# Where a convolution's running sum is kept: SBUF or a PSUM bank, in a decoder layer on one Trainium2 core

## The chip, the cores and the metric

One core of a Trainium2 chip runs the whole layer as one program. Five engines work side by side, each on its own queue in its own order: TensorE (PE) multiplies matrices and writes PSUM, VectorE (DVE) and ScalarE (ACT) do elementwise work and read and write both memories, GpSimd (POOL) does elementwise work in SBUF alone, and SyncE (SP) issues the transfers. PSUM has eight banks of 128 x 512 fp32. The metric is device time in microseconds (us) of one execution. The kernel before takes 3000.27 us (median of 3 runs, 2999.34 to 3004.11). A difference of under 0.2%, about 6 us, cannot be told from no change here.

## The reference

One decoder layer on 2048 tokens of width 1024. A normalised and modulated input is multiplied by one wide matrix, and the columns feed three mixers:

```python
h = rmsnorm(x, norm_mix_w[l]) * (1.0 + sc1) + sh1
proj = h @ w_in[l]
o_a = hgrn2_mixer(hq, hf, hi, hg, ...)     # gated linear recurrence, 4 heads of 128x128 state
o_b = dsa_mixer(sq, sk, sv, iq, ik, iw)    # index scores, top 256 keys, softmax attention
o_c = conv_module(cu, ...)                 # this change
mix = concat([o_a, o_b, o_c]) @ w_out[l];  x = x + g1 * mix
ff = square(relu(h2 @ mlp_w1[l])) @ mlp_w2[l];  x = x + g2 * ff
```

The convolution module is the part that is edited: `h = a * sigmoid(b)` on 256 channels, a causal depthwise convolution of 31 taps over the positions plus a bias, a LayerNorm over the channels, and a swish. So each output is a sum of 31 products of a shifted row with one weight per channel.

## The kernel before

The tokens go in four blocks of 512 (`NB`). For each block `in_block` runs 26 projection units: 23 of 24 matmuls 512 columns wide (L424) and 3 of 96 matmuls of 256 columns (L1290). Each operand is split into a high and a low part, so that a product is three matmuls. Nearly all units write one of two `mm` PSUM banks, which ACT and DVE take off. Then come the output projection of block 0 (L1314, `out_block`) and the MLP blocks, between which the other output projections lie. Call the matmuls of L424, L1290, L1314 and L1474 the wide ones: they are nearly all of PE's work.

Beside the projections run generators that are pumped a piece at a time by `step()`:

- `hgrn_gen`, the recurrence, one head of one block at a time, 16 in all, here numbered 0 to 15. A head is a chain: two score banks `pd` (L681, read at L685 and L687), six levels in each of which PE multiplies into a bank (L706, L714), DVE or ACT takes it into `at` (L708, L718) and DVE scales halves of q and k (L671, L672) that the next level reads; then a transpose of k (L728), the state update (L734, L739, L747), the outputs (L744, L746), a root mean square on ACT and POOL (L751, L252, L755), a transpose back (L759) and a last product on DVE (L761). All its banks have the tag `ax`.
- `conv_gen`, the convolution of one block, in two halves of 128 channels (`m`). Of the 31 taps, DVE adds 16 into `acc` (L585 starts it, L597 adds 15); the other 15 are multiplied by ACT, the first straight into `cside` (one buffer, L591) and 14 into `ctap` (one buffer, L594), which POOL adds to `cside` (L595). L602 adds the two sums. After both halves the LayerNorm takes an `ax` bank three times (L608, L620, L627).
- index scores, top-k and attention (L819 to L1024), and the modulation vectors (`ada_gen`, L196).

The PSUM banks in the first stage: two `mm`, two `at`, one `po`, and three rotating `ax` (`px["ax"]` is 3 there). In the MLP stage that pool is closed and its three banks are handed out again: one `ax` and two `ix`; the first user of each waits for the last reader of the bank's former tile.

The order of the instructions on each engine is not that of the source: a scheduler places them when the program is built, by the order of emission, by when buffers come free, and by its own estimate of durations. Each engine then runs its list strictly in order. So a change of a buffer moves instructions over the whole program.

Of the kernel before, what the change touches and what calls it, by code (L numbers as in the profile page):

```python
# [8 lines left out]
F32 = mybir.dt.float32  # L9
# [7 lines left out]
OP = mybir.AluOpType  # L17
# [3 lines left out]
P = 128  # L21
D = 1024
L = 2048
TB = 512
# [54 lines left out]
def trunk(ctx, tc, x, c, ada_w, ada_b, norm_mix_w, norm_mlp_w, w_in, hg_lb_logits,  # L79
# [3 lines left out]
    V, A, G, T = nc.vector, nc.scalar, nc.gpsimd, nc.tensor  # L83
# [14 lines left out]
    px = {"p": SP.enter_context(tc.tile_pool(name="psx", bufs=1, space=PSUM)), "ax": 3}  # L98
# [3 lines left out]
    def nm(s):  # L102
        uid[0] += 1
        return f"{s}_{uid[0]}"

    def dma(o, i):
        return nc.sync.dma_start(o, i)
# [5 lines left out]
        return pp.tile([P, 512], F32, tag="mm", bufs=2, name=nm("mm"))  # L113

    def ps_ax():
        return px["p"].tile([P, 512], F32, tag="ax", bufs=px["ax"], name=nm("ax"))

    def ps_ix():
        if px["ax"] == 3:
# [6 lines left out]
    def ps_xp(i):  # L126
        return {'0': ps_ax, '1': ps_mm, '2': ps_at, '3': ps_po}[XP[i]]()
# [3 lines left out]
    def ps_rot():  # L131
        turns[0] += 1
        return ps_mm() if turns[0] % 3 else ps_ax()
# [29 lines left out]
    crow = xp.tile([8, P], F32, tag="tf", bufs=2, name="crow")  # L163
    dma(crow, c[0].rearrange("(r p) -> r p", p=P))
    pt = ps_ax()
    T.transpose(pt[:, :8], crow, ident[:8, :8])
    cact = cst.tile([P, 8], F32, name="cact")
# [18 lines left out]
    def col(key, i=0, n=1):  # L186
        return cols[:, offs[key] + i:offs[key] + i + n]
# [62 lines left out]
    def rpow(dst, src, w, scale):  # L250
        G.tensor_scalar(dst, src, scale, EPS, op0=OP.mult, op1=OP.add)
        G.tensor_tensor(dst, dst, nhalf.to_broadcast([P, w]), OP.pow)  # L252
# [189 lines left out]
    hp = S1.enter_context(tc.tile_pool(name="hgrn", bufs=1))  # L442
# [9 lines left out]
    def st(tag, bufs, w=TB, dt=F32, shape=None):  # L452
        return hp.tile(shape or [P, w], dt, tag=tag, bufs=bufs, name=nm(tag))
# [126 lines left out]
    def conv_gen(b):  # L580
        accs = []
        for m in range(2):
            hc = conv[m]
            acc = hp.tile([P, TB], F32, tag=f"csg{m}", bufs=1, name=nm("cacc"))
            V.tensor_scalar(acc, hc[:, 0:TB], cvc[:, m, 0:1], col("cvb", m), op0=OP.mult, op1=OP.add)  # L585
            side = None
            for w in range(1, TAPS):
                if w % CT == 1:
                    if side is None:
                        side = hp.tile([P, TB], F32, tag="cside", bufs=1, name=nm("cside"))  # L590
                        A.mul(side, hc[:, w:w + TB], cvc[:, m, w:w + 1])  # L591
                    else:
                        tap = hp.tile([P, TB], F32, tag="ctap", bufs=CB, name=nm("ctap"))
                        A.mul(tap, hc[:, w:w + TB], cvc[:, m, w:w + 1])  # L594
                        G.tensor_tensor(side, side, tap, OP.add)  # L595
                else:
                    V.scalar_tensor_tensor(acc, hc[:, w:w + TB], cvc[:, m, w:w + 1], acc,  # L597
                                           op0=OP.mult, op1=OP.add)
                if w % 3 == 0:
                    yield 1300  # L600
            if side is not None:
                V.tensor_tensor(acc, acc, side, OP.add)  # L602
            accs.append(acc)
        yield 1200
        tot = st("cside", 1)
        G.tensor_tensor(tot, accs[0], accs[1], OP.add)
        pm = ps_xp(4)
        T.matmul(pm, o256.to_broadcast([P, P]), tot, start=True, stop=True)  # L608
        for m in range(2):
            V.tensor_tensor(accs[m], accs[m], pm, OP.subtract)  # L610
        sqs = []
        for m in range(2):
            sq = st("cu", 2)
            A.activation(sq, accs[m], AF.Square)
            sqs.append(sq)
        G.tensor_tensor(sqs[0], sqs[0], sqs[1], OP.add)
        yield 1500
        pv = ps_xp(5)
        for t in range(4):
            T.matmul(pv[:, t:t + 1], sqs[0][:, t * P:(t + 1) * P], ones[:, 0:1], start=True, stop=True)  # L620
        rc = hp.tile([P, 4], F32, tag="crs", bufs=1, name=nm("crs"))
        V.tensor_copy(rc, pv[:, :4])
        rpow(rc, rc, 4, 1.0 / 256.0)
        yield 1500
        rs = ps_xp(6)
        for t in range(4):
            T.matmul(rs[:, t * P:(t + 1) * P], rc[:, t:t + 1].to_broadcast([P, P]), ident, start=True, stop=True)  # L627
        for m in range(2):
            V.scalar_tensor_tensor(accs[m], accs[m], col("lnw", m), rs, op0=OP.mult, op1=OP.mult)
            sg = st("cu", 2)  # L630
            A.activation(sg, accs[m], AF.Sigmoid, bias=col("lnb", m))
            o = st("cu", 2)
            V.scalar_tensor_tensor(o, accs[m], col("lnb", m), sg, op0=OP.add, op1=OP.mult)
            dma(mx_d[b][6 + m], o)
        yield 3000
# [491 lines left out]
    def in_block(b, xts, nxt):  # L1127
        act = first_units(xts) if b == 0 else to_act(xts, a1, sh1, half if TM else None)
        for u, (pieces, ev, m) in enumerate(in_units):
# [38 lines left out]
            if ev is ev_ca and m == 1:  # L1168
                queues["conv"].append(conv_gen(b))
# [507 lines left out]
```

## Time and profile before

| | us |
|---|---|
| median of 3 runs | 3000.27 |
| the profiled execution | 3001.11 |
| its span, first to last instruction | 2999.4 |
| PE busy | 2810.5 (94%) |
| DVE busy | 1722.4 (57%) |
| ACT busy, POOL busy | 1297.8 (43%), 1265.8 (42%) |
| mean granted clock of PE | 0.972 |
| DVE in L597, 120 taps | 120.4 |
| POOL in L595, 112 taps | 164.3 |

PE is the busiest engine, so what counts is where PE stands idle or runs below its full clock. In a table by stretches of time, "us, busy (x)" gives for each engine the busy time and the count of instructions in the stretch, and "PEclk" the granted clock. A row of the waits says which PE instruction waited for which instruction of another engine: total, times, longest.

### The profile page before, as it was taken

Reading aid. Unit: us, or ns where it says so; the run is one execution under the profiler, and the core shown is the slowest. Engines: PE = TensorE matmul, PEld = TensorE weight load, DVE = VectorE, ACT = ScalarE, POOL = GpSimd, SP = SyncE. Lnnn points to the kernel's source line nnn. Section 1 sums busy time; section 2 is a strip of 40 time slices with the busy share of each in tenths; the row PEclk is TensorE's granted clock in tenths of the full one; section 3 lists DMA queues with packets and bytes.
Section 4 is the critical chain, followed back from the end, with each engine's and each line's share of the span. In section 5 each row is a group of like instructions: output and inputs, shape, how many; then the busy total and the mean of one; then the engine's idle time right before and its main releaser. Section 6 shows DMA issues by size and latency. Waiting matters only on the chain. (4 is left out here: it accounts for less than half of the span.)

```text
span 2999.4 us, 42837 instructions
## 1 busy us (share of the span) xinstructions
PE 2810.5 (94%) x14116; PEld 2325.2 (78%) x14116; DVE 1722.4 (57%) x3450; ACT 1297.8 (43%) x2706; POOL 1265.8 (42%) x1163
## 2 busy tenths in 40 slices
PE   6988989898899999999998999999999999999998
PEld 4877868786787877788776888877788888777777
DVE  7795487968446343747658646575944211244545
ACT  4445545435322324565546444443653333233333
POOL 7574143216313254566647422223532223334454
PEclk9999989999999998999998999999999999999999
DMA  8866656575644577899978966677786666676676
GB/s 280 273 203 210 214 185 203 188 238 181 210 167 152 180 253 230 255 296 285 294 234 271 313 218 202 218 219 227 248 290 208 220 223 213 213 269 229 225 235 210
DMA packets 428074, 688.61 MB, mean 230 GB/s; under 512 B 43383, under 2 KB 171452, under 8 KB 427836
## 3 DMA queue, kind: packets, MB, share of 16 engines
q1 hardware_dynamic: 427680, 685.67, 71.2%
q8 instruction: 112, 1.84, 0.3%
q14 instruction: 126, 1.03, 0.1%
q10 hardware_dynamic: 156, 0.07, 0.0%
HBM read 532.74 MB, written 152.84 MB: 229 GB/s over the span
## 5 line engine op out<-in xcount | busy, mean ns | idle before, releaser
L424 PE MATMUL mm<-ah,wk 128*128 128x512 f32 x1920 | 516.7, 402 | 15.6 <-DVE adrow L777 4.5
L424 PEld LDWEIGHTS mm<-ah,wk 128*128 128x128 f32 x1920 | 358.2, 191 | 90.0 <-DVE adrow L777 4.7
L318 POOL TENSOR_TENSOR wlo<-wraw,whi 128x512 fp32r<-128x512 f32 x210 | 290.2, 1402 | 168.5 <-ACT whi L317 104.7
L1008 POOL TENSOR_TENSOR pT<-L,pT 128x512 fp32r<-128x512 f32 (+3 forms) x160 | 198.0, 1239 | 295.7 <-ACT pT L1007 177.5
L826 DVE SCALAR_TENSOR_TENSOR s<-r,iw_s,s 128x512 f32<-128x512 f32 (+3 forms) x266 | 242.4, 911 | 112.9 <-ACT r L821 104.9
L424 PE MATMUL mm<-al,wk 128*128 128x512 f32 x960 | 266.3, 398 | 0.0
L978 DVE CUSTOM_DVE_ANT_0 L<-at,bias 128x512 f32<-128x512 f32 (+3 forms) x152 | 93.7, 619 | 219.6 <-PE at L976 180.7
L595 POOL TENSOR_TENSOR cside<-cside,ctap 128x512 f32<-128x512 f32 x112 | 164.3, 1467 | 109.9 <-ACT ctap L594 97.6
L424 PEld LDWEIGHTS mm<-al,wk 128*128 128x128 f32 x960 | 180.5, 192 | 36.5
L821 ACT ACTIVATE r<-ix 128x512 f32<-128x512 f32 (+3 forms) x256 | 133.0, 554 | 158.5 <-PE ix L819 117.8
L270 POOL TENSOR_TENSOR hl<-hr,hh 128x512 fp32r<-128x512 f32 x96 | 127.9, 1332 | 173.6 <-ACT hh L262 173.4
L1314 PE MATMUL mm<-wk,hh 128*128 128x512 f32 x640 | 198.6, 400 | 1.5 <-DMA wk<-wk_d 1.0
L424 PE MATMUL ax<-ah,wk 128*128 128x512 f32 x720 | 187.2, 393 | 1.4 <-ACT hc L1448 1.4
L317 ACT CAST whi<-wraw 128x512 fp32r<-128x512 f32 x210 | 121.3, 619 | 145.5 <-DMA wraw<-in_mlp_w_dram 46.6
L928 DVE TENSOR_SCALAR_CACHE_REDUCE cum<-s,ssm 128x384 bf16<-128x384 f32 (+13 forms) x112 | 165.4, 1477 | 10.4 <-POOL s L830 8.2
L424 PEld LDWEIGHTS ax<-ah,wk 128*128 128x128 f32 x720 | 134.1, 188 | 31.5 <-ACT hc L1448 1.9
L1006 ACT COPY L<-at 128x512 f32<-128x512 f32 (+3 forms) x160 | 83.0, 523 | 161.1 <-PE at L998 159.4
L1474 PE MATMUL mm<-wk,hc 128*128 128x512 f32 x588 | 147.7, 397 | 2.2 <-DVE acc L1482 2.1
L992 ACT ACTIVATE L<-L,nmx 128x512 f32<-128x512 f32 (+3 forms) x160 | 103.8, 651 | 104.8 <-DVE nmx L987 104.4
L1314 PEld LDWEIGHTS mm<-wk,hh 128*128 128x128 f32 x640 | 118.6, 189 | 28.2 <-DMA wk<-wk_d 1.8
L1474 PEld LDWEIGHTS mm<-wk,hc 128*128 128x128 f32 x588 | 109.6, 188 | 31.7 <-DVE acc L1482 5.7
L594 ACT ACTIVATE ctap<-hc,cvc 128x512 f32<-128x512 f32 x112 | 81.0, 723 | 107.4 <-POOL cside L595 106.9
(368 smaller groups left out, 6448.1 us busy)
## 6 DMA issues: line engine op xcount, KB each, us to landing
wk<-wk_d SPq DMA_DIRECT2D x776, 256.0 KB
wk<-wk_d SPq DMA_DIRECT2D x196, 512.0 KB
wk_d<-whi SPq DMA_DIRECT2D x210, 256.0 KB
wk_d<-wlo SPq DMA_DIRECT2D x210, 256.0 KB
wraw<-in_mlp_w_dram SPq DMA_DIRECT2D x68, 512.0 KB
kc<-sk_d SPq DMA_DIRECT2D x112, 256.0 KB
vc<-v_d SPq DMA_DIRECT2D x112, 256.0 KB
adw<-in_ada_w_dram SPq DMA_DIRECT2D x128, 128.0 KB
```

Source lines behind the costliest of these rows:

```text
L270: e.tensor_tensor(lo[:, i:j], src[:, i:j], hi[:, i:j].bitcast(F32), OP.subtract)
L317: A.copy(hi, src)
L318: G.tensor_tensor(lo, src, hi.bitcast(F32), OP.subtract)
L424: T.matmul(ps, ww[k], aa[k], start=(n == 0 and k0 == 0), stop=(n == len(order) - 1 and k1 == NK))
L595: G.tensor_tensor(side, side, tap, OP.add)
L821: A.activation(r[:, :w], ps[:, :w], AF.Relu, scale=32.0 ** -0.5)
L826: V.scalar_tensor_tensor(s[:, c0:c0 + w], r[:, :w], iw, s[:, c0:c0 + w], op0=OP.mult, op1=OP.add)
L928: V.tensor_scalar(dump, s, t, -AIM - i * STEP, op0=OP.is_ge, op1=OP.add, accum_out=d)
L992: A.activation(lt[:, :w], lt[:, :w], AF.Exp, bias=nmx, accum_out=sm[:, cb:cb + 1])
L1008: G.tensor_tensor(pT[:, :nt, 1], lv, pT[:, :nt, 0].bitcast(F32), OP.subtract)
L1314: T.matmul(ps, aa[f][:, tok * P:(tok + 1) * P], ww[i], start=(first and n == 0), stop=(last and n == 5))
L1474: T.matmul(bank[t], aa[:, k, t * P:(t + 1) * P], ww[k], start=(i in (0, 2, 4) and n == 0), stop=(n == 5), skip_group_check=True)
```

## The change

DVE's running sum of a half's taps is no longer an SBUF tile but a PSUM bank of a new tag `cx`, of which there is one. The sum of the two parts (L602) now reads that bank and writes an SBUF tile `total`, which the LayerNorm uses as it used `acc`. To make room, the recurrence and the LayerNorm rotate over two `ax` banks instead of three. The first tap and the 15 others of a half write the bank, the 15 also read it; the shifted rows `hc` stay in SBUF. The counts of instructions on DVE, PE, POOL and in the transfers are the same. In the MLP stage nothing of the source differs, but its three banks are now laid over two `ax` and one `cx`.

```diff
     def ps_ax():
-        return px["p"].tile([P, 512], F32, tag="ax", bufs=px["ax"], name=nm("ax"))
+        return px["p"].tile([P, 512], F32, tag="ax", bufs=min(px["ax"], 2), name=nm("ax"))
+
+    def ps_cx():
+        return px["p"].tile([P, 512], F32, tag="cx", bufs=1, name=nm("cx"))
...
         for m in range(2):
             hc = conv[m]
-            acc = hp.tile([P, TB], F32, tag=f"csg{m}", bufs=1, name=nm("cacc"))
+            acc = ps_cx()
             V.tensor_scalar(acc, hc[:, 0:TB], cvc[:, m, 0:1], col("cvb", m), op0=OP.mult, op1=OP.add)
...
-            if side is not None:
-                V.tensor_tensor(acc, acc, side, OP.add)
-            accs.append(acc)
+            total = hp.tile([P, TB], F32, tag=f"csg{m}", bufs=1, name=nm("cacc"))
+            V.tensor_tensor(total, acc, side, OP.add)
+            accs.append(total)
```

In the lists of the changed kernel the line numbers are 3 higher from L117 on (L597 is L600, L602 is L605, L728 is L731).

The first place is DVE's list at the convolution of the second block (tokens 512 to 1023). `cacc_4701` and `cacc_5240` are the running sums of the two halves, `hc` the shifted rows, `cvc` the weights. Before:

```order
L585 TENSOR_SCALAR cacc_5240<-hc_4690,cvc,cols 128x512
L597 SCALAR_TENSOR_TENSOR cacc_4701<-hc_4607,cvc,cacc_4701 128x512
L597 SCALAR_TENSOR_TENSOR cacc_5240<-hc_4690,cvc,cacc_5240 128x512
L597 SCALAR_TENSOR_TENSOR cacc_4701<-hc_4607,cvc,cacc_4701 128x512
L597 SCALAR_TENSOR_TENSOR cacc_5240<-hc_4690,cvc,cacc_5240 128x512
L597 SCALAR_TENSOR_TENSOR cacc_4701<-hc_4607,cvc,cacc_4701 128x512
L597 SCALAR_TENSOR_TENSOR cacc_5240<-hc_4690,cvc,cacc_5240 128x512
```

In the changed kernel `cx_4703` and `cx_5243` are the two sums, `cacc_5241` is `total`, `at`, `q`, `k` belong to the recurrence, and `slo` to a projection:

```order
L540 TENSOR_TENSOR slo_5051<-mm_5021,shi_5050 128x512
L605 TENSOR_TENSOR cacc_5241<-cx_4703,cside_4705 128x512
L711 COPY_PREDICATED at_4290<-lmask,ax_4509 128x64x4
L674 TENSOR_TENSOR q_3940<-q_3940,fb_4405 128x4x16x4
L675 TENSOR_TENSOR k_3815<-k_3815,fb_4405 128x64x4
L588 TENSOR_SCALAR cx_5243<-hc_4692,cvc,cols 128x512
```

Before, the taps of the two halves alternate. Now the second half's first tap (L588) stands behind the first half's total (L605), because there is one `cx` bank; it is so in all four blocks.

The second place is PE's list where the output projection of block 0 has ended and the MLP begins. `x_21..` are the normalised rows of block 0 that L278 transposes for the MLP; `ax` rows belong to head 15, the last of the recurrence. Before, the end of that head stands among these transposes:

```order
L728 MATMUL ax_11660<-ident,k_11084 128x128 x4
L278 MATMUL mm_11793<-ident,x_2171_11217 128x128
L278 MATMUL mm_11793<-ident,x_2172_11219 128x128
L278 MATMUL mm_11793<-ident,x_2173_11221 128x128
L278 MATMUL mm_11793<-ident,x_2174_11223 128x128
L278 MATMUL mm_11804<-ident,x_2171_11217 128x128
L278 MATMUL mm_11804<-ident,x_2172_11219 128x128
L278 MATMUL mm_11804<-ident,x_2173_11221 128x128
L278 MATMUL mm_11804<-ident,x_2174_11223 128x128
L734 MATMUL ax_11699<-v_10629,kt_11665 128x128 x4
L744 MATMUL ax_11708<-v_10629,at_11204 128x128
```

In the changed kernel it stands behind four units of the MLP (L427 is the wide matmul), and the unit behind it writes the MLP's own `ax` bank:

```order
L427 MATMUL mm_12091<-ah_11839,wlo_12031 128x512
L731 MATMUL ax_11668<-ident,k_11092 128x128 x4
L737 MATMUL ax_11707<-v_10636,kt_11673 128x128 x4
L747 MATMUL ax_11716<-v_10636,at_11212 128x128
L749 MATMUL ax_11716<-S_st_197,q_11170 128x128
...
L762 MATMUL ax_11738<-ident,hu_11727 128x128 x4
L427 MATMUL ax_11977<-ah_11762,whi_11912 128x512
```

So no wide matmul and no transpose of the input stands any more between L731 and L762 of head 15; the rows left out are six more of L747 and L749.

## The prediction

> **What bounds the kernel now.** I read the page's head, then the busy time by stretches, then PE's waits, then the groups of DVE and POOL, and last the timeline where the MLP begins.
>
> ```profile
> span 2999.4 us, 42837 instructions
> PE 2810.5 (94%) x14116; PEld 2325.2 (78%) x14116; DVE 1722.4 (57%) x3450; ACT 1297.8 (43%) x2706; POOL 1265.8 (42%) x1163
> ```
>
> PE bounds the whole: 189 us of the span are PE's idle time. The convolution runs in four short stretches, and the table of busy time, cut at their ends, shows another bound there. Columns: stretch, length, then busy us and count for PE, PEld, DVE, ACT, POOL, then the granted clock.
>
> ```profile
> 121.00:186.00 65.00, 53.85 (x240) 42.17 (x240) 65.00 (x100) 28.65 (x51) 44.24 (x33) 0.91 0.62 188
> 186.00:389.00 203.00, 185.52 (x1141) 161.53 (x1140) 118.96 (x324) 103.96 (x232) 78.70 (x88) 0.96 0.69 218
> 389.00:444.00 55.00, 42.06 (x197) 32.57 (x196) 54.16 (x91) 27.70 (x51) 29.97 (x26) 0.84 0.53 166
> 444.00:673.00 229.00, 208.91 (x1279) 181.78 (x1278) 169.12 (x465) 102.93 (x241) 61.16 (x73) 0.96 0.66 209
> 673.00:732.00 59.00, 48.09 (x243) 38.40 (x242) 54.76 (x91) 30.14 (x52) 37.38 (x25) 0.91 0.50 160
> 732.00:927.00 195.00, 181.55 (x1088) 157.57 (x1088) 81.67 (x186) 66.42 (x162) 48.40 (x48) 0.96 0.60 194
> 927.00:972.00 45.00, 38.95 (x188) 31.95 (x188) 44.72 (x60) 15.60 (x25) 20.52 (x16) 0.92 0.43 136
> 972.00:1117.00 145.00, 142.84 (x834) 123.40 (x833) 57.92 (x116) 47.31 (x113) 58.34 (x51) 0.98 0.63 205
> 1117.00:1146.00 29.00, 20.02 (x121) 16.17 (x119) 20.52 (x38) 10.68 (x19) 13.25 (x14) 0.71 0.45 158
> ```
>
> The convolution's stretches are rows 1, 3, 5 and 7: 224 us in which DVE is busy 218.6 (98%), PE 182.9, idle 41.1 (18%), at a clock of about 0.90. In the four stretches between (772 us) DVE is busy 427.7 (55%), PE 718.8, idle 53.2 (7%), at 0.96. So with the taps, DVE is what ends last, and PE pays: at the rate of the other stretches it would idle 15.4 us, so 25.6 are too many, and the lower clock (means weighted by PE's busy time) costs 182.9 x (1 - 0.896/0.964) = 12.9. Together **38.5 us is what a saturated DVE costs PE**. PE's waits over the first 1125 us name the path, the recurrence's chain through DVE. A tap stands in DVE's list between two links of this chain, and PE, in order too, holds its wide matmuls behind the next level. Columns: total, times, longest:
>
> ```profile
> PE ax L706 <- DVE k L672: 15.4, 9, 4.8
> PE ax L714 <- DVE k L672: 11.9, 8, 2.8
> PE ax L706 <- DVE q L671: 8.2, 3, 4.6
> PE ax L746 <- DVE sa L739: 6.5, 7, 3.0
> PE ax L728 <- DVE k L672: 4.8, 2, 4.6
> ```
>
> **The taps.** Their durations (minimum, median, maximum, ns), and the groups with their means:
>
> ```profile
> L597 DVE SCALAR_TENSOR_TENSOR cacc<-hc,cvc,cacc x120: 722/741/1875, 121.7 to 970.4; 128x512 f32<-128x512 f32 x120
> L629 DVE SCALAR_TENSOR_TENSOR cacc<-cacc,cols,ax x8: 732/740/749, 305.5 to 1103.4; 128x512 f32<-128x512 f32 x8
> L595 POOL TENSOR_TENSOR cside<-cside,ctap x112: 1262/1302/6887, 122.2 to 1002.1; 128x512 f32<-128x512 f32 x112
> L597 DVE SCALAR_TENSOR_TENSOR cacc<-hc,cvc,cacc 128x512 f32<-128x512 f32 x120 | 120.4, 1020 | 0.3
> L602 DVE TENSOR_TENSOR cacc<-cacc,cside 128x512 f32<-128x512 f32 x8 | 6.3, 783 | 0.0
> L610 DVE TENSOR_TENSOR cacc<-cacc,ax 128x512 f32<-128x512 f32 x8 | 5.1, 681 | 10.8 <-PE ax L608 10.8
> L585 DVE TENSOR_SCALAR cacc<-hc,cvc,cols 128x512 f32<-128x512 f32 x8 | 5.5, 682 | 0.0
> L287 DVE TENSOR_SCALAR ah<-mm,a,sh 128x512 fp32r<-128x512 f32 x48 | 38.2, 802 | 20.3 <-ACT tf L283 20.3
> ```
>
> A tap with both tensors in SBUF takes 741 ns at the median but 1020 on the mean; POOL's adds beside it are 1302 and (164.3 us over 112) 1467. L629 is the same operation with one tensor in PSUM, and never leaves 732 to 749. So a tap on the bank should take 0.741 us: 120 x (1.020 - 0.741) = 33.5 us, and L602, now like L610, 8 x (0.783 - 0.681) = 0.8: **34.3 us less DVE work**. POOL may gain up to 112 x 0.165 = 18.5 us, but the chain ACT to POOL of one half is long anyway, so I count nothing. The first tap moves between 0.68 and L287's 0.80: 1 us at most.
>
> [...]
>
> No row shows DVE writing PSUM, or reading and writing one bank. The bounds are 0.68 us (L610) and the slowest tap, 1.875; at 1.02 the gain is nil, at 1.875 DVE does 103 us more. I take 0.741, the row of the same operation.
>
> **Where the taps stand.** Before, both halves' 30 taps lie in the saturated stretch. With one bank the second half starts behind the first half's total, which waits for POOL's side sum; so about 60 x 0.741 = 44.5 us of DVE work leave these stretches for those behind them. What is a us of DVE worth to PE? Between 55% and 98% of DVE load lie 38.5 us of loss over 0.43 x 224 = 96 us of DVE time: 0.40. On that line moving work is neutral, and 34.3 saved is worth **13.7 us**. If the loss comes only close to saturation, moving counts too: the stretches fall to (218.6 - 120.4 + 44.5)/224 = 64%, and 38.5 x 34/43 = 30 us are the ceiling.
>
> **Two banks.** Inside a level the third bank is idle: a level's bank is read (L708) before the scaling that the next level needs. It bites at a head's change: L759's bank must be read by L761 before the next head's second `pd` bank is free, 0.75 us in the chain, 16 x 0.75 = 12 us if nothing covers it. In PE's built order the recurrence does fall back against the wide matmuls: head 3 starts behind 977 of them and not 897, head 8 behind 2056 (1920), head 12 behind 2952 (2812). PE does the same work in another order, so this is free while buffers last: `f` of a head needs the head three before it ended, and in that order the nearest case had 144 wide matmuls to spare and has 72, some 17 us at 8 in 1.9 us. I take nothing, and keep 0 to 12.
>
> **The start of the MLP.** What falls back must end here.
>
> ```profile
> 1117.26 0.63 PE L1314 MATMUL mm<-wlo,mh 128*128 128x512 f32 x2
> ...
> 1125.39 0.55 POOL L252 TENSOR_TENSOR rs<-rs,nhalf 128x1 f32<-128x1 f32 x1
> ...
> 1133.52 0.75 DVE L1375 TENSOR_SCALAR x<-x,rs 128x1024 f32<-128x1024 f32 x1
> ...
> 1138.82 1.11 PE L728 MATMUL ax<-ident,k 128*128 128x128 f32 x4
> ...
> 1141.31 1.06 PE L734 MATMUL ax<-v,kt 128*128 128x128 f32 x8
> ...
> 1145.55 0.39 PE L746 MATMUL ax<-sa,q 128*128 128x128 f32 x2
> ...
> 1145.97 0.50 PE L424 MATMUL mm<-ah,whi 128*128 128x512 f32 x1
> ...
> 1147.49 1.02 POOL L252 TENSOR_TENSOR hrs<-hrs,nhalf 128x4 f32<-128x4 f32 x1
> ...
> 1148.54 1.14 ACT L755 ACTIVATE hu<-ax,hrs 128x128 f32<-128x128 f32 x4
> ...
> 1153.78 0.75 DVE L761 SCALAR_TENSOR_TENSOR r<-ax,cols,gate 128x512 f32<-128x512 f32 x1 [6.94 <-PE ax L759]
> 1157.50 1.98 PE L424 MATMUL ax<-ah,whi 128*128 128x512 f32 x8
> ```
>
> From 1117.9 to 1146 PE has no wide matmul. The last row block's scale is ready at 1125.9, but DVE normalises it at 1133.5, behind levels of head 15. In the changed order the four L1375 stand ahead of that head: 7.6 us gained. But its end, L728 to L761, now has nothing of PE's beside it: 1138.8 to 1149.7 (L755), then about 0.6 for L759 (an estimate from L734's row) and 0.75 for L761, 12.2 us, of which about 5.3 are PE's own (L728 1.1, L734 1.1, eight pairs of 0.39); 6.9 lost. Net 0.
>
> **The sum.** 3001.11 is the profiled run, 1.7 over its span and 0.84 over the median. 3001.1 - 13.7 = 2987.4; less the 0.84, **2987 us**.
>
> **Rivals.**
> - *Saturation counts alone* (chance 0.13): 30 us gained, 2970. For it: DVE at 65.00 of 65. Against it: PE also waits for DVE in stretches where that is half idle.
> - *No change* (0.22): DVE gets lighter, but PE's list is in another order and waits as long at other places, or the bank write costs what the sharing cost: 3000, between 2995 and 3005. For it: the L706 and L714 waits also occur between the convolutions.
> - *Slower* (0.21): the recurrence, short of a bank, falls back so far that its end lies bare. Price: 16 x 0.75 = 12 us of bank waits and 6.9 at the MLP, less half of 13.7: 3012. It decides once L681 waits for L761 on PE, or the third MLP unit for L759. Against it: 72 wide matmuls of slack.
> [...]
>
> **Chances.** My forecast, 2980 to 2994, has 0.44. Taking all cases, the range is 2965 to 3011. A measurement here tells 0.2%, 6 us, from nothing; faster 0.55, same 0.21, slower 0.24.
>
> **What would show it.** L600 at a mean near 0.74 us with a narrow spread; POOL's L598 nearer 1.3; DVE well under 98% in the stretches with taps, and PE's idle time there under 18% and its clock over 0.9. Wrong if L600 is above 0.9, if PE's idle time up to the first MLP unit is as before, or if more than 10 us of idle PE stand around head 15's L731 to L762.

## The result, and the profile after

The changed kernel takes **2969.72 us** (median of four runs, 2959.47 to 2972.15) against 2999.81 for the kernel before: a ratio of 0.9888, 95% interval 0.9866 to 0.9911, faster by 30 us by the medians and 1.1% by the ratio. The forecast was 2987, in a range from 2965 to 3011. The profiled run of the changed kernel is the fastest of the four (2959.47, 10 us under their median), so differences between the two profiles come out near 42 us where the medians give 30.

In the rows of the changed kernel the tap is L600, the half's first tap L588, GpSimd's side add L598 and the sum of the parts L605. The head of its page:

```profile
span 2957.7 us, 42853 instructions
PE 2796.6 (95%) x14116; PEld 2310.3 (78%) x14116; DVE 1680.2 (57%) x3450; ACT 1297.0 (44%) x2704; POOL 1241.9 (42%) x1163
```

PE's idle time fell from 188.9 to 161.1 us, its busy time by 13.9. DVE is busy 42.2 us less, POOL 23.9 less. The group of GpSimd's adds (busy us, mean ns), and then every instruction on the bank (minimum, median, maximum, ns):

```profile
L598 POOL TENSOR_TENSOR cside<-cside,ctap 128x512 f32<-128x512 f32 x112 | 150.3, 1342 | 100.5 <-ACT ctap L597 88.3 <-ACT cside L594 9.9 <-DMA wk<-wk_d 1.1
```

```profile
L600 DVE SCALAR_TENSOR_TENSOR cx<-hc,cvc,cx x120: 730/748/757, 122.9 to 941.6; 128x512 f32<-128x512 f32 x120
L588 DVE TENSOR_SCALAR cx<-hc,cvc,cols x8: 793/802/814, 122.0 to 926.0; 128x512 f32<-128x512 f32 x8
L605 DVE TENSOR_TENSOR cacc<-cx,cside x8: 674/680/684, 174.0 to 958.6; 128x512 f32<-128x512 f32 x8
```

None of the 120 taps is longer than 757 ns; before, their mean was 1020 and the longest 1875. The adds beside them went from a mean of 1467 to 1342. The prediction's stretches with taps, from the first tap of a block to its last (columns as in the prediction: stretch, length, busy us of PE, PEld, DVE, ACT, POOL, granted clock), are now:

```profile
122.00:203.00 81.00, 73.68 (x381) 61.31 (x381) 73.15 (x174) 44.64 (x86) 58.44 (x50) 0.96 0.72 228
371.00:441.00 70.00, 61.88 (x311) 48.82 (x310) 63.30 (x115) 41.46 (x81) 40.55 (x39) 0.98 0.68 217
642.00:711.00 69.00, 59.55 (x286) 47.55 (x285) 63.66 (x122) 38.60 (x74) 37.96 (x35) 0.95 0.66 210
890.00:942.00 52.00, 51.81 (x259) 43.25 (x258) 41.16 (x69) 25.34 (x49) 28.89 (x24) 1.00 0.62 197
```

In these 272 us DVE is busy 241.3, still 89%, but PE idles only 25.1, 9% where it was 18%, at a clock of 0.95 to 1.00.

Where the time was won: cut both executions at the same wide matmuls (10284 in each; from the 96th to the 576th, the 1152nd to the 1344th, the 2016th to the 2112th, the 2880th to the 2976th). The four pieces hold most of the four convolutions, 107 of the 120 taps before. They give, before:

```profile
75.86:211.93 136.07, 120.22 (x611) 100.89 (x611) 110.01 (x209) 60.37 (x117) 84.20 (x65) 0.94 0.78 244
383.63:466.63 83.00, 68.22 (x334) 54.91 (x333) 74.86 (x130) 42.51 (x84) 45.38 (x40) 0.90 0.61 191
677.75:723.08 45.33, 34.73 (x181) 27.60 (x180) 41.58 (x68) 21.80 (x40) 28.94 (x19) 0.89 0.48 154
938.88:973.14 34.26, 28.21 (x137) 22.60 (x135) 34.04 (x48) 11.92 (x21) 13.95 (x10) 0.90 0.38 120
```

and after:

```profile
75.49:194.46 118.97, 112.79 (x603) 95.13 (x603) 88.11 (x206) 62.03 (x119) 77.58 (x65) 0.99 0.89 276
364.66:435.01 70.35, 62.23 (x315) 49.59 (x313) 59.85 (x109) 38.57 (x78) 38.19 (x39) 0.98 0.70 220
649.18:684.60 35.42, 31.70 (x146) 24.85 (x144) 32.52 (x68) 22.44 (x47) 18.45 (x17) 0.95 0.58 186
900.80:928.07 27.27, 27.08 (x137) 22.75 (x136) 17.74 (x34) 14.94 (x32) 14.45 (x13) 1.00 0.57 177
```

Together 298.7 us became 252.0: 46.7 won in these pieces, and 5 given back elsewhere. Of the 46.7, 29.1 are PE's idle time (length less PE's busy time: 47.3 before, 18.2 after), and 17.6 its busy time, whose granted clock went from 0.89 to 0.94 up to 0.95 to 1.00. Part of this is work that moved: after the change the pieces hold 74 taps, since the second halves come later, and 62 fewer of PE's small matmuls. Still, the stretches with taps idle less although they are longer, so the gain lies where the prediction put it; it is over twice the forecast size (30 us by the medians against 13.7).

PE's waits over the first 1125 us, as the prediction showed them of before (waiting line, released by; total, times, longest). After:

```profile
PE mm L427 <- ACT k L647: 11.5, 3, 5.6
...
PE ax L709 <- DVE k L675: 8.4, 10, 2.2
...
PE ax L749 <- DVE sa L742: 3.5, 5, 1.5
...
PE ax L684 <- DVE r L764: 3.0, 7, 1.5
...
PE ax L709 <- DVE q L674: 2.2, 2, 1.1
...
PE ax L731 <- DVE k L675: 1.9, 3, 0.8
PE ax L717 <- DVE k L675: 1.5, 3, 0.7
```

The five rows on the recurrence's chain that the prediction quoted were 46.8 us; the same five are 17.5 here. The bank wait that the two banks bring (L684 for L764) is 3.0. These five rows are a sign and not a measure of the time: in the runs below they are 34.6 in a kernel that is 44 us faster than the one before (no adds), and 35.5 in one that is 19 us slower (two banks alone).

One place shows what a tap was. The timeline of before, DVE and POOL side by side (start, duration):

```profile
135.09 1.32 POOL L595 TENSOR_TENSOR cside<-cside,ctap 128x512 f32<-128x512 f32 x1 [0.84 <-ACT ctap L594]
135.36 1.59 DVE L597 SCALAR_TENSOR_TENSOR cacc<-hc,cvc,cacc 128x512 f32<-128x512 f32 x1
136.37 3.12 POOL L318 TENSOR_TENSOR wlo<-wraw,whi 128x512 fp32r<-128x512 f32 x2
...
137.21 1.15 DVE L671 TENSOR_TENSOR q<-q,fb 128x256 f32<-128x256 f32 x1
138.29 1.48 DVE L672 TENSOR_TENSOR k<-k,fb 128x256 f32<-128x256 f32 x1
```

The tap begins 0.27 us behind the add and ends 0.54 behind the add's end, 0.85 us later than 0.74 would have taken it: it stood for most of the add. The next POOL operation (L318) meets the recurrence's own two products, L671 and L672, here 1.15 and 1.48 us; L672 is L675 in the changed kernel, and takes 0.41 in the next rows. Over all taps of before, the 38 beside which GpSimd has no instruction take 728 to 753 ns; the 68 that have one of its adds beside them take 1182 on the mean, up to 1875, and make 30 of the 33.6 us that the taps stand over 741. Why the two stretch each other, no row shows. The same kind of place after:

```profile
131.77 1.30 POOL L598 TENSOR_TENSOR cside<-cside,ctap 128x512 f32<-128x512 f32 x1
131.85 0.74 DVE L600 SCALAR_TENSOR_TENSOR cx<-hc,cvc,cx 128x512 f32<-128x512 f32 x1
...
132.83 0.51 DVE L674 TENSOR_TENSOR q<-q,fb 128x256 f32<-128x256 f32 x1
133.27 0.41 DVE L675 TENSOR_TENSOR k<-k,fb 128x256 f32<-128x256 f32 x1
```

The tap runs inside the add, neither is lengthened, and when the recurrence's products come the add is nearly over. The 71 taps of the changed kernel that have an add alone beside them take 730 to 757 ns.

### The profile page after: what moved, and what is told of

Read it like the earlier page. It is cut to its first block, busy times and chain, and to the rows that moved or that the text cites. A ratio compares the mean times of both kernels' runs of the same rounds, so it can differ in the third digit from the quotient of the medians.

```text
span 2957.7 us, 42853 instructions
## 1 busy us (share of the span) xinstructions
PE 2796.6 (95%) x14116; PEld 2310.3 (78%) x14116; DVE 1680.2 (57%) x3450; ACT 1297.0 (44%) x2704; POOL 1241.9 (42%) x1163
## 4 chain that ended last, share of the span: by engine, by line
PE 38%; DMA 5%; DVE 4%; POOL 2%; issue 1%; ACT 1%; SPq 0%; POOLq 0%; DVEq 0%; ACTq 0%
PE mm L1317 10%; PE mm L427 8%; PE ax L427 6%; PE ax L1317 5%; PE mm L1477 4%; PE po L1013 1%; PE at L979 1%; PE at L1001 1%; DMA wk<-wk_d 1%; PE at L1317 1%; PE ix L822 1%; DMA tr<-in_mlp_w_dram 1%; DMA xo<-x_d 1%; DMA wraw<-in_mlp_w_dram 1%; DMA out_dram<-xo 1%
## 5 line engine op out<-in xcount | busy, mean ns | idle before, releaser
L427 PE MATMUL mm<-ah,wk 128*128 128x512 f32 x1920 | 517.3, 401 | 15.1 <-ACT k L647 5.9
L427 PEld LDWEIGHTS mm<-ah,wk 128*128 128x128 f32 x1920 | 358.3, 191 | 90.0 <-ACT k L647 6.9
L427 PE MATMUL mm<-al,wk 128*128 128x512 f32 x960 | 262.1, 395 | 0.0
L427 PEld LDWEIGHTS mm<-al,wk 128*128 128x128 f32 x960 | 178.9, 190 | 36.0
L598 POOL TENSOR_TENSOR cside<-cside,ctap 128x512 f32<-128x512 f32 x112 | 150.3, 1342 | 100.5 <-ACT ctap L597 88.3
L427 PE MATMUL ax<-ah,wk 128*128 128x512 f32 x720 | 187.0, 393 | 1.5 <-ACT hc L1451 1.5
L427 PEld LDWEIGHTS ax<-ah,wk 128*128 128x128 f32 x720 | 134.0, 188 | 31.2 <-ACT hc L1451 1.9
L1317 PE MATMUL ax<-wk,hh 128*128 128x512 f32 x384 | 123.4, 400 | 0.9 <-DMA wk<-wk_d 0.5
```

The costliest lines, as they stand in the source:

```text
L427: T.matmul(ps, ww[k], aa[k], start=(n == 0 and k0 == 0), stop=(n == len(order) - 1 and k1 == NK))
L1317: T.matmul(ps, aa[f][:, tok * P:(tok + 1) * P], ww[i], start=(first and n == 0), stop=(last and n == 5))
```

## The experiments

Four explanations were set against one another. **Work**: PE is held up by the amount of VectorE's work in these stretches, so any us less is worth something between 0.4 (the prediction's line) and 1. **Order**: the second half's taps moved behind the first's total, and PE's list changed. **Chain**: GpSimd's shorter adds release ScalarE, which has one tap buffer and waits in order. **Collisions**: VectorE and GpSimd stretch each other, and the stretching costs, on whichever instruction it falls. Ratios are against the kernel before, run on the same chip.

**The banks alone (order).**

```
 before, ps_ax:
-        ... tag="ax", bufs=px["ax"]
+        ... tag="ax", bufs=min(px["ax"], 2)
```

> The kernel before with two rotating banks for the recurrence and nothing else; the convolution's sum stays in SBUF. If the taps' change gave the 30 us, two banks alone give nothing: 2995 to 3015, and the end of head 15, bare as in the changed kernel, costs up to 11 us there. The rival, that the changed order of PE's work (which two banks also bring) gave the gain, expects 2970 to 2985.

3018.7 us, ratio 1.0063 (1.0046 to 1.0079): 19 us slower, 4 more than the top of what was expected. Two banks, and the order that PE's list takes with them, give nothing; alone they cost.

**The order of the halves, without the bank.**

```
 after, conv_gen:
-            acc = ps_cx()
+            acc = hp.tile([P, TB], F32, tag="csg1", bufs=1, name=nm("cacc"))
...
-            total = hp.tile([P, TB], F32, tag=f"csg{m}", bufs=1, name=nm("cacc"))
+            total = acc if m else hp.tile([P, TB], F32, tag="csg0", bufs=1, name=nm("cacc"))
```

> The changed kernel with its running sum in one SBUF tile for both halves, in place of the bank: the second half still begins behind the first one's total, two banks stay, but the taps again have two inputs in SBUF. If the moved half is what counts, the time is near the changed kernel's: 2970 to 2980. If the shorter taps count (L600 at 748 against 1020), it is near the kernel before or above: 2995 to 3010, with the taps' mean back at 0.95 to 1.05 us, or somewhat lower where fewer of POOL's adds stand beside them.

3002.55 us, ratio 0.9999 (0.9986 to 1.0013). Moving the half is worth the 19 us that the two banks cost, and no more; the rest of the way to the changed kernel, 33 us (0.0111 of 3000), is the bank's. The taps were longer than before:

```profile
L600 DVE SCALAR_TENSOR_TENSOR cacc<-hc,cvc,cacc 128x512 f32<-128x512 f32 x120 | 129.8, 1082 | 1.4
```

**Less work, with the contention left as it is.** Four of the 15 taps that VectorE adds in each half are left out, once in the kernel before and once in the kernel with one SBUF sum:

```
+                    if w not in (4, 12, 20, 28):
                         V.scalar_tensor_tensor(acc, hc[:, w:w + TB], cvc[:, m, w:w + 1], acc, ...)
```

> The kernel before with 4 of the 15 VectorE taps of each half left out (32 instructions of a mean 1.02 us in all, 32.6 us; this part of the convolution is missing), and no other change. If a us of VectorE in these stretches is worth a us to PE, 2968 to 2972; by the 0.40 of the prediction, 2987; if it is hidden, 3000.

> One SBUF tile for both halves' sum and two banks (2995 to 3007), with 4 of 15 VectorE taps of each half left out (this part of the convolution is missing): 32 instructions of 1.08 us, 34.6 us less VectorE work, the contention stays. If the order of the halves decides what a us of VectorE is worth, 2970 to 2978 (0.8 a us, as from this kernel to the changed one). If the long taps are the cost, leaving some out gives as little as in the order before: 2994 to 3000.

2996.82 us, ratio 0.9981 (0.9970 to 0.9992), in the one; 3006.32, ratio 1.0017 (1.0001 to 1.0034), in the other. Over a quarter of these taps is gone, and 6 us are won or 5 lost. The groups, first from the kernel before, then from the one with one sum:

```profile
L598 DVE SCALAR_TENSOR_TENSOR cacc<-hc,cvc,cacc 128x512 f32<-128x512 f32 x88 | 87.5, 1009 | 0.2
```

```profile
L601 DVE SCALAR_TENSOR_TENSOR cacc<-hc,cvc,cacc 128x512 f32<-128x512 f32 x88 | 103.6, 1177 | 1.2
```

In the second the mean of the remaining taps rose from 1082 to 1177. DVE's whole busy time fell by 23.3 us in the one (1722.4 to 1699.1) and by 24.7 in the other (1730.3 to 1705.6), about 0.75 for each tap left out and not the 1.02 and 1.08 that they had taken: the standing stayed, on other instructions. The work explanation does not fit here, and neither does the prediction's way of counting; a us of VectorE that is saved by doing less is worth a quarter of a us in the one kernel and nothing in the other.

**More and less work on the bank.** The same four taps done twice, or left out, in the changed kernel:

```
-                    V.scalar_tensor_tensor(acc, hc[:, w:w + TB], ...)
+                    for _ in range(2 if w in (4, 12, 20, 28) else 1):
+                        V.scalar_tensor_tensor(acc, hc[:, w:w + TB], ...)
```

> The changed kernel with 4 VectorE taps of each half done twice (32 more instructions of 0.748 us, 23.9 us; these taps count double in the output). If a us of VectorE is worth a us to PE there, 2992 to 2996; by 0.40, 2979; if the moved half has left VectorE room, 2970.

> The changed kernel with 4 of the 15 VectorE taps of each half left out (32 instructions of 0.748 us, 23.9 us of VectorE work; this part of the convolution is missing). With SBUF sums, leaving the same taps out gave -6 us in the order before, and +4 us beside the one SBUF sum. If VectorE's work as such still holds PE up now that the taps meet nothing (by the 14 us that 23.9 us more cost), 2956. If only the stretching by collisions counts, nothing again: 2966 to 2972.

Twice: 2984.11 us, ratio 0.9946 (0.9929 to 0.9962), 17 us more than the changed kernel's 0.9888 for 24 us of taps. That is more a us than the prediction's 0.40, and the work explanation would have it so; but the standing rose as well, by 18 us in the table further down, and no run separates the two. Left out: ratio 0.9916 (0.9900 to 0.9932), five runs from 2973 to 2989; that is 8 us **more** as well, though the two intervals just overlap. Neither explanation had expected a loss. The profile shows where the saved 23.9 us went:

```profile
PE 2817.4 (94%) x14116; PEld 2329.9 (78%) x14116; DVE 1687.7 (56%) x3418; ACT 1302.0 (44%) x2708; POOL 1234.0 (41%) x1163
```

```profile
L676 DVE TENSOR_TENSOR k<-k,fb 128x256 f32<-128x256 f32 x96 | 62.7, 653 | 0.0
```

With 32 instructions fewer, DVE is busy 7.5 us *longer* (1687.7 against 1680.2). The taps left are as short as in the changed kernel (749 ns); others got longer, among them the recurrence's k product, whose mean went from 592 ns in the changed kernel,

```profile
L675 DVE TENSOR_TENSOR k<-k,fb 128x256 f32<-128x256 f32 x96 | 56.8, 592 | 0.0
```

to 653, and PE's waits for that chain came back:

```profile
PE ax L710 <- DVE k L676: 11.9, 9, 3.4
...
PE ax L718 <- DVE k L676: 9.0, 7, 3.3
PE ax L685 <- DVE r L765: 8.8, 4, 5.3
```

One reading is that a tap on the bank keeps GpSimd's adds away from the recurrence. The records do not show it: of the 224 products L674 and L675, 35 have an add beside them in the changed kernel and 32 of their counterparts here, the adds got shorter (1323 ns against 1342), and of the 11 us that the products gained 8 lie beside GpSimd's other work. This profile is of an execution of 2989.49 us and the changed kernel's of one of 2959.47, 30 us apart where the ratios give 8, so a part of what differs lies between executions. Why less work cost time here is open.

**Half on the bank.** The first half's sum in `cx`, the second's in SBUF, so that the halves alternate as before:

```
 after, conv_gen:
-            acc = ps_cx()
+            acc = hp.tile([P, TB], F32, tag="csg1", ...) if m else ps_cx()
...
-            total = hp.tile([P, TB], F32, tag=f"csg{m}", ...)
+            total = acc if m else hp.tile([P, TB], F32, tag="csg0", ...)
```

> The changed kernel with only the first half's running sum in the bank; the second half's is one SBUF tile, so that the halves no longer share a buffer and stand side by side as before, and only half of the taps (60) have two inputs in SBUF. So far: one SBUF tile for both halves and two banks gave 2995 to 3007 (as before), the bank 2970, both halves side by side with two banks 3019. If the shorter taps are what counts, half of them give half the way from 3019 to 2970: 2990 to 3000. If one half behind the other is needed as well, it stays at 3010 to 3020.

2988.1 us, ratio 0.9968 (0.9945 to 0.9991): 28 us better than two banks alone, about half of the way to the changed kernel. Both kinds of tap stand in one execution, between the same neighbours. Where one of GpSimd's adds alone is beside them, 33 on the bank take 745 ns on the mean and 28 in SBUF 978:

```profile
L600 DVE SCALAR_TENSOR_TENSOR cx<-hc,cvc,cx x60: 729/744/797, 121.1 to 927.5; 128x512 f32<-128x512 f32 x60
L600 DVE SCALAR_TENSOR_TENSOR cacc<-hc,cvc,cacc x60: 717/743/1780, 133.4 to 935.2; 128x512 f32<-128x512 f32 x60
```

**Three banks with the sum in one of them.**

```
 after, ps_ax:                          conv_gen:
-        ... bufs=min(px["ax"], 2)     -            acc = ps_cx()
+        ... bufs=px["ax"]             +            acc = ps_ax()
```

> The changed kernel with three rotating banks as before, and the running sum in one of them (no bank of its own): the recurrence has two while a sum lies there and three at other times, and the end of head 15 need not lie bare. If two banks cost the recurrence what they cost alone (19 us), much of it comes back: 2945 to 2960. If they cost nothing beside the sum in PSUM, 2965 to 2975. If the rotation makes a level wait for a whole sum, slower than 2980.

2966.59 us, ratio 0.9896 (0.9864 to 0.9928): not to be told from the changed kernel. A third bank, which the recurrence has whenever no sum lies in it, is worth nothing that shows.

**GpSimd's adds taken away.** From the kernel before, once without the adds, and once with two fills of the tap's buffer in their place:

```
 e8:                                                e11:
-  G.tensor_tensor(side, side, tap, OP.add)        -  G.tensor_tensor(side, side, tap, OP.add)
                                                   +  G.memset(tap, 0.0)
                                                   +  G.memset(tap, 0.0)
```

> The kernel before without GpSimd's 112 adds of the side taps (these taps are missing from the output), nothing else moved: VectorE's taps keep two SBUF inputs, but what they met beside them is gone. If GpSimd's adds are what lengthens them, the taps' mean falls from 1.02 to 0.74 to 0.80 us, 26 to 34 us less VectorE work. Time: by the 0.17 us per us that leaving taps out showed, 2994 to 2996; if a long tap itself (up to 1.9 us) is what PE waits for, 2965 to 2975.

> The kernel before with each of GpSimd's 112 side adds replaced by two fills of the tap's buffer with zeros (the side taps are missing from the output): the chain from ScalarE to GpSimd and back over the one buffer stays, at a similar length, but GpSimd reads nothing there. Leaving out the adds gave 2954. If the collisions are the cost, the taps fall to 0.75 to 0.85 us and the time to 2950 to 2965. If the chain over GpSimd is the cost, 2990 to 3000.

2954.12 us, ratio 0.9853 (0.9818 to 0.9888), without; 2955.15, ratio 0.9836 (0.9815 to 0.9857), with the fills. VectorE does all its taps from SBUF in both, in the order before and with three banks. The fills keep the loop from ScalarE to GpSimd and back, though shorter (118.6 us of POOL, where the adds were 164.3); ScalarE waits 76.0 us for them, and it costs nothing that shows:

```profile
L594 ACT ACTIVATE ctap<-hc,cvc 128x512 f32<-128x512 f32 x112 | 81.0, 723 | 76.5 <-POOL ctap L596 76.0
...
L595 POOL MEMSET ctap<- 128x512 f32 x112 | 59.6, 532 | 89.2 <-ACT ctap L594 89.0
L596 POOL MEMSET ctap<- 128x512 f32 x112 | 59.0, 527 | 5.1
```

A fill, which writes SBUF and reads nothing, stretched no tap here: the 76 taps that have only fills beside them take 722 to 758 ns. Two taps, the first beside a fill and the second beside L318:

```profile
130.25 0.73 DVE L598 SCALAR_TENSOR_TENSOR cacc<-hc,cvc,cacc 128x512 f32<-128x512 f32 x1
130.35 0.52 POOL L595 MEMSET ctap<- 128x512 f32 x1
...
133.34 3.45 POOL L318 TENSOR_TENSOR wlo<-wraw,whi 128x512 fp32r<-128x512 f32 x2
...
135.58 1.76 DVE L598 SCALAR_TENSOR_TENSOR cacc<-hc,cvc,cacc 128x512 f32<-128x512 f32 x1
```

The taps' means are 834 ns without the adds and 801 with the fills, not 741, since GpSimd's other work still meets them, as L318 does in the last two rows (the tap takes 1.76 us). GpSimd also has less to do in both, 162 and 57 us of its busy time, and what that alone is worth no run separates.

**ScalarE released from the adds (chain).** The side taps take the two `cu` buffers in place of the one `ctap`:

```
 before, conv_gen:
-  tap = hp.tile([P, TB], F32, tag="ctap", bufs=CB, name=nm("ctap"))
+  tap = st("cu", 2)
```

> The kernel before with two buffers in place of one for ScalarE's side taps, so that ScalarE, which works in order, can write the next tap while GpSimd still adds the last; the sum stays in SBUF. L594 waited 106.9 us for GpSimd's adds. If these waits, and what they hold up behind them on ScalarE, are what the long adds cost, then half of the gain at least: below 2985. If the cost is that VectorE and GpSimd stretch each other, the adds and the taps stay as long as before (taps 1.0 us, adds 1.4 to 1.5) and the time stays at 2995 to 3005.

3015.86 us, ratio 1.0040 (1.0024 to 1.0055): slower. ScalarE's wait fell from 106.9 to 66.9 us, and the taps' mean rose from 1020 to 1113 ns:

```profile
L594 ACT ACTIVATE cu<-hc,cvc 128x512 f32<-128x512 f32 x112 | 79.9, 723 | 67.0 <-POOL cside L595 66.9
...
L597 DVE SCALAR_TENSOR_TENSOR cacc<-hc,cvc,cacc 128x512 f32<-128x512 f32 x120 | 132.0, 1113 | 0.2
```

Forty us less waiting on ScalarE won nothing, and with the fills 76.0 us of it cost nothing that shows: the chain does not explain the gain.

**An attempt at a better kernel.** In the changed kernel the end of head 15 (L731 to L762) stands on PE behind four products of the MLP with nothing beside it. Here the first four take `mm` banks only, and the end stands among their matmuls:

```
 after, ps_rot:                        and behind px["ax"] = AXB:
+        if px.get("hold", 0):         +    px["hold"] = 4
+            px["hold"] -= 1
+            return ps_mm()
```

> The changed kernel with one more edit: the first four products of the MLP take their banks from mm alone, so that PE's list has the end of head 15 (L734 to L765 here) among their matmuls and not bare behind them. From the 3600th to the 3648th wide matmul the changed kernel had lost 9.3 us against the kernel before. If that was the bare end, 2960 to 2964; if the wait only moves behind, 2970.

2974.94 us, ratio 0.9913 (0.9894 to 0.9932): no gain, if anything a loss. By the 3648th wide matmul its profile is 2.5 us ahead of the changed kernel's, by the 3800th 8.6 behind: what the start gained was lost right behind it, and why is open. No version that does the whole layer's work was clearly faster than the changed kernel.

**All runs on one scale.** For each DVE instruction up to the MLP's first product, take what it lasted beyond the bound of the shortest tenth of its kind (same source line, operation and shape, over all the kernels here), and add up. This *stretch* is an estimate, worked out from the records of the profiled runs. Beside it, how many us of taps were added or left out (32 by 0.73 or 0.75), and the time by the ratio:

```
kernel                        stretch  plain work   time against before
before                          164        0              0
two banks alone                 161        0            +19
two tap buffers                 165        0            +12
one SBUF sum                    164        0              0
fewer taps, before              162      -23             -6
fewer taps, one SBUF sum        161      -23             +5
half on the bank                137        0            -10
more taps, after                134      +24            -16
fewer taps, after               145      -24            -25
sum in one of three banks       138        0            -31
changed, MLP starts on mm       124        0            -26
changed                         116        0            -34
no adds                          86        0            -44
fills for adds                   78        0            -49
```

A line through zero has a slope of 0.61 us of time per us of stretch, with a scatter of 9 us about it; the plain work beside it has no effect that these runs could tell. The two kernels with the least stretch, taken alone, give 44 us for 78 (no adds) and 49 for 86 (fills), that is 0.56 and 0.57 a us; by these the changed kernel's 48 us less are worth 27 to 28. That the stretch goes with the time over all these kernels is a correlation; that most of it comes of GpSimd's adds, and that time is won when they are gone, is what the runs without them show.

## Why the prediction was right, and where it was mis-sized

**The taps: right.** L600's mean is 748 ns, forecast 741; the narrow spread was forecast too. L605 took 680, L588 802, both as the rows of before had it. A tap that reads and writes the bank takes 7 ns more than one in SBUF (748 against 741, both medians; the 38 in SBUF beside which GpSimd has nothing take 740 on the mean). L600 above 0.9 us, by which the prediction would have been wrong, did not come.

**What a us of DVE is worth: the step that failed.** The sum had 34.3 us of DVE at 0.40, that is 13.7; the medians give 30. The time lies outside the forecast's own 2980 to 2994, and inside the range of 2965 to 3011 only because that range also covered a rival; that it was hit is in part luck. Two errors lie in the sum. First, the amount: DVE is busy 42.2 us less, which at 0.40 would still be only 17. By the table the stretch is 48 less, 32.7 of it in the taps and some 16 in other instructions, about 5 each in the index scores' sums (L826) and in the recurrence's two products, ten fewer of which stand in the counted time. The prediction counted POOL's gain as nothing and no other instruction's either. Second, the price: the line from 55% to 98% of DVE load took all DVE time as alike. Leaving out 23 us of taps moved the time by -6 and +5 us; where stretch is gone, 0.56 to 0.61 us went with each us of it. DVE's 98% was a sign, not the cause: a stretched instruction counts as busy while it stands (L597, with a median of 741 ns, is busy 120.4 us in 120 taps), and at 89% after the change PE idles half as much (9% for 18%). "Saturation counts alone", at 2970 with a chance of 0.13, named the right time for a wrong reason: it too would have had fewer taps, and the moved half, win much.

**Moving half of the taps: neutral, as forecast**, but only with two banks: with them, and the sum in SBUF, halves one behind the other take 19 us less than alternating ones. A gain as large as the ceiling of 30 us came, but not from moving, on which that ceiling rested: with the sum in SBUF the moved half leaves the time where it was (0.9999).

**Two banks: 0 taken out of 0 to 12, right here, in part by luck.** L684 waits 3.0 us for L764, and three banks shared with the sum change nothing (0.9896 against 0.9888). Alone, though, they cost 19 us, above the bound that the prediction kept, and with SBUF sums it took the moved half to win that back; the prediction had neither term. Why it is 19, with a stretch no greater than before, is open; PE's list is in another order in that kernel, and two kernels with other orders and the same stretch (two tap buffers, one SBUF sum) differ by 12 as well.

**The start of the MLP: net 0 forecast, some 4 lost.** The timeline of after:

```profile
1070.88 0.62 PE L1317 MATMUL mm<-wlo,mh 128*128 128x512 f32 x2
...
1083.31 0.75 DVE L1378 TENSOR_SCALAR x<-x,rs 128x1024 f32<-128x1024 f32 x1
...
1091.53 1.97 PE L281 MATMUL mm<-ident,x 128*128 128x128 f32 x8 [3.21 <-ACT tf L286]
...
1098.97 0.78 PE L427 MATMUL mm<-ah,whi 128*128 128x512 f32 x1
```

The last normalisation (L1378) stands ahead of the head and no longer behind it, as forecast; but the 7.6 us did not come of it. From the last product of the output projection to the first of the MLP it is 27.5 us, before 28.1: the transposes' copies on ScalarE (L281 for L286) and two levels of the head are next. The bare end cost 3.7 us of idle PE (34.08 less 30.39 below), forecast 6.9; PE's idle time from the 3456th to the 3648th wide matmul is 12.9, before 9.0:

```profile
1098.97:1133.05 34.08, 30.39 (x171) 24.86 (x169) 7.61 (x18) 13.63 (x32) 15.87 (x14) 0.98 0.75 247
```

**Slower** asked that bank waits decide; they were 3.0 us. **No change** rested on PE waiting elsewhere as long, or on a write of the bank as dear as what the taps had stood beside GpSimd's adds: a tap on the bank takes 748 ns. PE's waits for projections did grow (L427 for ACT's k 11.5, before 6.6), against 29 us less on the recurrence's chain.

What stays open is how PE comes to pay half a us and more for a us of stretch, and next to nothing for a us of taps left out, though 24 us of added taps cost 17. The recurrence's two products, for which PE waits, are nearly as long in sum in both kernels (134.1 us before, 130.2 after), so it is not mainly by their own standing; the taps that stood between them are what got shorter. No run set a stretch on one kind of instruction alone.

## What to carry to other kernels

Where VectorE is nearly full (98% here) and one of its instructions has a maximum over twice its median (1875 ns and 741), look at what GpSimd does at that moment before counting the work: here 23 us of work left out moved the time by 6 us at most, and a change that took some 48 us of standing away won 30. So try such a sum in a PSUM bank, if one can be had: here its taps took 748 ns on the mean, and 1020 in SBUF in the kernel before. And read a busy share of 98% together with the spread of its instructions, since standing was counted as busy: 0.28 us a tap here (1020 ns on the mean less 741).

## What the hardware showed that was not expected

An instruction of VectorE with one tensor in SBUF that reads and writes the same PSUM bank, 128x512 in fp32, took 748 ns in the changed kernel, and 120 of them lie between 730 and 757. The first tap, a product and a sum with constants, was dearer into the bank: 802 ns at the median, where the same operation into SBUF took 542 in the kernel before:

```profile
L585 DVE TENSOR_SCALAR cacc<-hc,cvc,cols x8: 521/542/1507, 120.9 to 936.9; 128x512 f32<-128x512 f32 x8
```

GpSimd's fill of 128x512 took 0.53 us, and the 76 taps that met only fills were not stretched (722 to 758 ns); its add took 1.26 us at its shortest, and a tap that met an add up to 1.1 longer (1875 ns, where the median is 741). Less work on an engine need not leave it less busy: with 32 instructions fewer VectorE was busy 1687.7 us in one execution, against 1680.2 in one of the changed kernel.
